# Banded attention scores of two block pairs issued back to back, with one projection bank less

## The chip, the cores and the metric

The kernel runs on one core of one Trainium2 chip. The metric is the device time of one execution in microseconds; the figure before is the median of three runs, 1133.69 us.

## The reference, cut to what matters

One decoder layer over 2048 positions of width 1024. A normalised and modulated input is projected once into the operands of two attention branches; each branch output is gated, and both go through one output projection.

```python
h = rms_norm(x, g_pre) * (1 + scale) + shift
qa, ka, va, fa, za, qb, kb, vb, zb = split(h @ w_in)
oa = forgetting_attention(qa, ka, va, fa + b_fgate) * silu(za)      # 8 heads, causal, forget-gate bias
qb, kb = rope(qb), rope(kb)
ob = sliding_window_sink_attention(qb, kb, vb, sinks) * silu(zb)    # 8 heads, 2 key heads, window 128
y = concat(oa, ob) @ w_out
x = x + gate * rms_norm(y, g_post)
```

The change lies in branch B. There, every block of 128 queries looks at its own 128 keys and the 128 before it, masked to a band of 128; a learned "sink" score joins each row's softmax.

## The kernel before, in words

Everything on TensorE is done in 16-bit pieces: an operand is split into a high and a low half, and a product is three matmuls (high by high, high by low, low by high). The order of all instructions is written by hand: each engine runs its own instructions in the order in which the program issues them, and waits where it needs another's result.

The time falls into three parts. Up to about 140 us the input is normalised, transposed and projected. From 140 to 400 us runs the **banded stage**, where branch B's attention is mixed with projections of both branches. After it come branch A's attention and the output projection.

**The filler: projection units.** `punits` is a list of small pieces of projection work. `fill(n)` (line 1185) takes the next n; before each it runs the `events` booked for that position with `at_slice`. A group of 8 units makes one 128x512 result in one bank of PSUM: 24 matmuls of 512 columns (line 361: queries of branch B, `wh_qb`, and gates, `wh_zb`), or 48 of 256 columns (line 379: values of branch A, `wh_va`). At the group's end the result is taken out by ScalarE and then VectorE: L406 and L402 for a gate, L807 and L812 for a query, L385 and L389 for values. These are put off with `after(n, f)`, which runs f at the n-th next `tick()`.

**Banks.** `bk` holds three PSUM tiles of 128x512 f32. `bank(True)` takes the one longest unused and holds it; `release` gives it back once the VectorE step is issued.

**The pairs.** A `Pair(j, i)` is two neighbouring query blocks of one pair of heads; `windows` lists 32 of them, eight for each of the four head pairs j. A pair goes through:
- `scores` (L940 to L949): 12 matmuls of 64 rows. The two heads sit in rows 0 to 63 and 64 to 127, so that two matmuls run side by side. They write a tile `pss` of two banks from the pool `ps_s`, which has one buffer.
- `maxima` (L951 to L963): VectorE masks the scores (L956), puts in the sink (L958), takes the row maximum (L961, L963). Where a head pair starts, it first fills the missing block (L955).
- `exps` (L965 to L971): ScalarE's exponentials, the last reader of `pss`.
- `turn` (L973 to L996): four transposes (L977) into `pxb`, then a split by ScalarE (L986) and VectorE (L987) and four band cuts by GpSimd (L991, L993).
- `pv` (L998 to L1015): the product with the values, L1005, into `pob` of the pool `ps_pv`, one buffer of one bank; at the next tick `out_` (L1011, VectorE) reads it out.

The loop of line 1220 goes over the pairs. In step n it issues `maxima` of pair n, some units, `turn` of pair n-1, a tick, `exps` of pair n, units, a tick, `pv` of pair n-2, units, a tick, units, and last `scores` of pair n+1.

**Two small products use a bank of `bk` in passing.** `sums` (L892) adds up the forget gates: matmuls L896 and L897, held until a copy by VectorE (L900) three units later. `const_turn` (L763) turns a table of constants: matmul L766 and a ScalarE copy (L767) at the next tick. Its place, 40 units before the stage's end, is directly behind a `pv`.

**PSUM in all.** Eight banks: ahead of the banded stage three for `bk` and five for `ps_x`; in it three for `bk`, two for `ps_s`, one each for `ps_t` and `ps_pv`, one unused; after it `bk` grows to five.

Of the kernel before, what the change touches and what calls it, by code (L numbers as in the profile page):

```python
# [10 lines left out]
F32 = mybir.dt.float32  # L11
# [8 lines left out]
P = 128  # L20
# [4 lines left out]
CH = 512  # L25
# [18 lines left out]
def hybrid_layer(  # L44
# [23 lines left out]
    PSUM = bass.MemoryType.PSUM  # L68
    dram = ctx.enter_context(tc.tile_pool(name="dram", bufs=1, space=DRAM))
    bkx = ExitStack()  # L70
    ps_bk = bkx.enter_context(tc.tile_pool(name="ps_bk", bufs=1, space=PSUM, reuse_waits="tile"))
    psx = ExitStack()
    ps_x = psx.enter_context(tc.tile_pool(name="ps_x", bufs=5, space=PSUM, reuse_waits="tile"))

    const = ctx.enter_context(tc.tile_pool(name="const", bufs=1))
# [7 lines left out]
    def sm(n, tag):  # L83
        return small.tile([P, n], F32, tag=tag, name=tag)
# [95 lines left out]
        return kap  # L180


    bk = [ps_bk.tile([P, CH], F32, name=f"bk{n}") for n in range(3)]
    held, order_ = set(), [0, 1, 2]

    def bank(hold=False):
        n = next(n for n in order_ if n not in held)
        order_.remove(n)
        order_.append(n)
        if hold:  # L190
            held.add(n)
        return n

    def release(n):
        held.discard(n)
        order_.remove(n)
        order_.append(n)
# [4 lines left out]
    def after(n, f):  # L202
        late.append([n, f])

    def tick():
        now = [f for n, f in late if n <= 1]
        late[:] = [[n - 1, f] for n, f in late if n > 1]
        for f in now:
            f()
# [534 lines left out]
    fx, abp = {}, None  # L744
# [17 lines left out]

    def const_turn():  # L763

        px = bk[bank()][:]
        PE.matmul(px[0:XR, 0:P], fx["cst"][:], identh[:], start=True, stop=True)  # L766
        after(1, lambda: A.activation(fx["crow"][64:XR, :], px[64:XR, 0:P], AF.Copy))  # L767

# [13 lines left out]
    def swa_pool(name, bufs, **kw):  # L782
        return swa.enter_context(tc.tile_pool(name=name, bufs=bufs, reuse_waits="tile", **kw))
# [94 lines left out]
    def gates():  # L878

        nf = fap.tile([P, NB, 8], F32, name="nf")  # L880
        V.tensor_scalar(nf[:], fl[:], -1.0, None, op0=ALU.mult)
        na = fap.tile([P, NB, 8], F32, name="na")
        V.tensor_tensor(na[:], fl[:], nf[:], op=ALU.min)

        def logs():
            A.activation(na[:], na[:], AF.Exp)
            A.activation(na[:], na[:], AF.Ln, bias=1.0)

        def total():
            V.scalar_tensor_tensor(nf[:], nf[:], 0.0, na[:], op0=ALU.max, op1=ALU.add)  # L890

        def sums():  # L892
            lsf = nf[:].rearrange("p t h -> p (t h)")
            held_ = bank(True)
            pc = bk[held_][:]
            PE.matmul(pc[:, 0:P], triu[:], lsf, start=True, stop=True)  # L896
            PE.matmul(pc[:, P:2 * P], ones[:], lsf, start=True, stop=True)  # L897
            yield
            cm = fap.tile([P, 2, NB, 8], F32, name="cm")
            V.tensor_copy(cm[:].rearrange("p a t h -> p (a t h)"), pc[:, 0:2 * P])  # L900
            release(held_)

            inn = na[:].rearrange("p (g r) h -> p g r h", g=4)
            blk = cm[:, 1].rearrange("p (g r) h -> p g r h", g=4)
            V.memset(inn[:, :, 0, :], 0.0)
            V.tensor_copy(inn[:, :, 1, :], blk[:, :, 0, :])
            for r in (2, 3):
                V.tensor_tensor(inn[:, :, r, :], inn[:, :, r - 1, :], blk[:, :, r - 1, :], op=ALU.add)
            yield
            tot = fap.tile([P, 4, 8], F32, name="tot")  # L910
            V.memset(tot[:, 0, :], 0.0)
            V.tensor_tensor(tot[:, 1:4, :], inn[:, 0:3, 3, :], blk[:, 0:3, 3, :], op=ALU.add)
            for g in (2, 3):
                V.tensor_tensor(tot[:, g, :], tot[:, g, :], tot[:, g - 1, :], op=ALU.add)
            yield
            V.tensor_tensor(inn, inn, tot[:].unsqueeze(2).broadcast_to([P, 4, 4, 8]), op=ALU.add)
            V.tensor_tensor(csum[:].rearrange("p h t -> p t h"), cm[:, 0], na[:],
                            op=ALU.add)

        after(1, logs)  # L920
        after(3, total)
        fx["sums"] = sums()

    ab = {}

    def qb_units(j, ci):
        def finish(stg):
            ab[j, ci] = stg

        return proj_units(f"qb{j}", ci, evac_rope(ci, finish, None))  # L930
# [128 lines left out]
    def at_slice(n, f):  # L1059
        events.setdefault(n, []).append(f)  # L1060
# [53 lines left out]
    add("qb0", qb_units(0, 1))  # L1114
    add(*others[6])
    N_PRO = len(punits)
    for n in range(4):
        at_slice(N_PRO + 20 + 3 * n, lambda: next(fx["sums"], None))
    qbs = [(f"qb{c_ // 4}", qb_units(c_ // 4, c_ % 4)) for c_ in range(2, 16)]
    n_o = 7  # L1120
    for n, (key, us) in enumerate(qbs):
# [4 lines left out]
        n_o = lim  # L1126
    N_SWA = len(punits)
    at_slice(N_SWA - 40, const_turn)
    for us in va_units(1, 2):
        add("va23", us)  # L1130
# [51 lines left out]
    windows = [Pair(j, i) for j in range(4) for i in range(0, NB, 2)]  # L1182
    pos = [0]

    def fill(n, each=None):

        for _ in range(n):
            for f in events.pop(pos[0], []):
                f()
            punits[pos[0]]()  # L1190
            pos[0] += 1
            if each:
                each()
# [8 lines left out]
    with swa_order:  # L1202
        fill(N_PRO - 4, tick2)
        psx.close()
        sws = swa_pool("sws", 2)
        ptp = swa_pool("ptp", 1)
        ps_s = swa_pool("ps_s", 1, space=PSUM)
        ps_t = swa_pool("ps_t", 1, space=PSUM)
        ps_pv = swa_pool("ps_pv", 1, space=PSUM)
        wsp = swa_pool("wsp", 2)  # L1210
        wss, wst = sm(16, "a_m"), sm(2, "wst")
        wsq = {}
        base = N_PRO
        NW = len(windows)
        windows[0].scores()
        windows[0].maxima()
        fill(2, tick2)
        windows[0].exps()
        fill(2, tick2)
        for n, wd in enumerate(windows):  # L1220
            goal = base + (N_SWA - base) * (n + 1) // NW
            todo = goal - pos[0]
            part = [todo * (m + 1) // 4 - todo * m // 4 for m in range(4)]
            tick()
            if n:
                wd.maxima()
            fill(part[0])
            if n:
                windows[n - 1].turn()
            tick()  # L1230
            if n:
                wd.exps()
            fill(part[1])
            tick()
            if n > 1:
                windows[n - 2].pv()
            fill(part[2])
            tick()
            fill(part[3])
            if n + 1 < NW:  # L1240
                windows[n + 1].scores()

            if n:
                A.activation(wsq[n - 1][:], wsq[n - 1][:], AF.Square, accum_out=wss[:, (n - 1) % 16:(n - 1) % 16 + 1])
            if n == 16:
                V.tensor_reduce(wst[:, 0:1], wss[:], axis=AX.X, op=ALU.add)
            wsq[n] = wsp.tile([P, 2 * P], F32, tag="wsq", name="wsq")
            SP.dma_start(wsq[n][:], w_out0[n // 4 * P:(n // 4 + 1) * P, n % 4 * 2 * P:(n % 4 + 1) * 2 * P])
        tick()
        fill(5)  # L1250
        windows[NW - 1].turn()
        tick()
        fill(5)
        windows[NW - 2].pv()
        tick()
        fill(6)
        windows[NW - 1].pv()
        tick()
        tick()
        A.activation(wsq[NW - 1][:], wsq[NW - 1][:], AF.Square, accum_out=wss[:, 15:16])  # L1260
        V.tensor_reduce(wst[:, 1:2], wss[:], axis=AX.X, op=ALU.add)
        wsum = sm(1, "w_mx2")
        V.tensor_reduce(wsum[:], wst[:], axis=AX.X, op=ALU.add)
# [6 lines left out]
    def fox_pool(name, bufs, **kw):  # L1270
        return fox.enter_context(tc.tile_pool(name=name, bufs=bufs, reuse_waits="tile", **kw))
# [1 line left out]
    ps_st = fox_pool("ps_st", 1, space=PSUM)  # L1273
    ps_po = fox_pool("ps_po", 1, space=PSUM)
    ps_bx = fox_pool("ps_bx", 1, space=PSUM)
    bk += [ps_bx.tile([P, CH], F32, name=f"bk{n}") for n in (3, 4)]
    order_ += [3, 4]
    foxl, foxo = ExitStack(), ExitStack()
    op_ = foxl.enter_context(tc.tile_pool(name="opa", bufs=2, reuse_waits="tile"))
    stp = foxl.enter_context(tc.tile_pool(name="stpa", bufs=3, reuse_waits="tile"))  # L1280
# [585 lines left out]
```

## Time and profile before

| what | value |
|---|---|
| median of 3 runs (lowest, highest) | 1133.69 us (1133.3, 1134.17) |
| the profiled execution's own time | 1133.33 us |
| its span, first to last instruction | 1131.6 us |
| TensorE busy | 1111.3 us, 98% |
| VectorE busy | 906.7 us, 80% |
| ScalarE busy | 657.8 us, 58% |
| GpSimd busy | 224.6 us, 20% |

PE is TensorE, PEld its weight loads, DVE is VectorE, ACT is ScalarE, POOL is GpSimd. In the rows of the timeline the first number is the start in us from the span's start, the second how long the row lasts, then come engine, source line, operation, the tiles (out<-in), the shape and, behind x, how many instructions the row merges; a bracket gives idle time of the engine before the row and what ended it. The ends of matmuls are modelled, so the pace of TensorE is read from starts. In the chain of waits a row says how long the chain stayed on one piece of work.

### The profile page before, as it was taken

The page shows a single profiled execution, that of the slowest core. Times are in us where ns is not written, and L with a number is a line of the kernel's source. Part 1 is how long each engine was busy: PE and PEld are TensorE (multiplying, and loading weights), DVE is VectorE, ACT ScalarE, POOL GpSimd, SP SyncE. Part 2 cuts the span into 40 slices and gives each one's busy share as a digit, 9 for nine tenths or more (in the row PEclk, how much of TensorE's full clock was granted, in tenths as well). Part 3 has the DMA queues.
Part 4 walks back from the last instruction along what each step waited for, and adds up shares of the span by engine and source line. Part 5 has one row for each costly group of instructions (what it writes and reads, how often), then busy time and mean ns, then how long its engine had stood idle before and what let it go on. Part 6 is the DMA issues. An engine that isn't in the chain of part 4 may idle for free.

```text
span 1131.6 us, 25123 instructions
## 1 busy us (share of the span) xinstructions
PE 1111.3 (98%) x9854; PEld 652.4 (58%) x9854; DVE 906.7 (80%) x1988; ACT 657.8 (58%) x1145; POOL 224.6 (20%) x341
## 2 busy tenths in 40 slices
PE   8899999999999999999999999999999999999997
PEld 3566555677756855555555555655555555544444
DVE  8897488878787568798998989989887998766673
ACT  3974355555555412766767677676666879533331
POOL 3111145555556410010100111001000000100000
PEclk9999999999999999999999999999999999999999
DMA  9854434413333142234232333215312246697643
GB/s 365 276 155 96 92 92 90 92 53 92 83 81 95 31 98 53 62 99 44 59 75 69 92 65 78 49 48 73 77 32 60 73 140 178 136 251 191 202 129 112
DMA packets 124365, 119.83 MB, mean 106 GB/s; under 512 B 65977, under 2 KB 101858, under 8 KB 124246
## 3 DMA queue, kind: packets, MB, share of 16 engines
q1 hardware_dynamic: 113374, 85.73, 28.4%
q0 software_dynamic: 10720, 32.46, 12.7%
q8 instruction: 77, 1.26, 0.5%
q14 instruction: 42, 0.34, 0.1%
q10 hardware_dynamic: 152, 0.04, 0.0%
HBM read 64.49 MB, written 25.18 MB: 79 GB/s over the span
## 4 chain that ended last, share of the span: by engine, by line
PE 81%; DVE 10%; DMA 4%; ACT 2%; issue 2%; POOL 0%; SPq 0%; DVEq 0%; POOLq 0%; ACTq 0%
PE bk L361 31%; PE bk L1646 13%; PE bk L379 7%; PE sta L1415 5%; PE sta L1414 5%; PE bk L1365 5%; PE poa L1440 3%; PE poa L1441 3%; PE poa L1438 3%; PE bk L854 2%; DMA wa<-in_w_ada_dram 2%; PE pss L948 2%; PE pob L1005 1%; PE px L453 1%; DVE pha L1428 1%
## 5 line engine op out<-in xcount | busy, mean ns | idle before, releaser
L1421 ACT ACTIVATE p<-sta,lift,scl_qk 128x1024 f32<-128x1024 f32 (+2 forms) x160 | 171.9, 1074 | 129.7 <-PE sta L1415 76.9
L361 PE MATMUL bk<-hT,wh_qk 128*128 128x512 f16 x768 | 196.4, 378 | 0.0
L1428 DVE TENSOR_TENSOR pha<-p,pha 128x1024 f16<-128x1024 f32 (+2 forms) x160 | 168.9, 1056 | 0.9 <-ACT pha L1425 0.9
L1646 PE MATMUL bk<-wohl,oz 128*128 128x512 f16 x744 | 163.6, 379 | 1.8 <-DVE oz L1596 1.6
L1368 DVE TENSOR_REDUCE a_m<-bk 128x1 f32<-128x512 f32 x192 | 130.2, 685 | 38.3 <-PE bk L1365 37.8
L1425 ACT ACTIVATE pha<-p 128x1024 f16<-128x1024 f32 (+2 forms) x160 | 147.9, 924 | 4.8
L1646 PEld LDWEIGHTS <-oz 128*128 128x128 f16 x744 | 70.6, 98 | 85.3 <-DVE oz L1596 2.6
L1438 PE MATMUL poa<-vt,pha 128*128 128x65 f16 x1088 | 116.3, 193 | 0.4 <-DVE ona L1447 0.4
L1440 PE MATMUL poa<-vt,pha 128*128 128x64 f16 x1088 | 116.3, 194 | 0.0
L1441 PE MATMUL poa<-vt,pha 128*128 128x65 f16 x1088 | 115.9, 192 | 0.4 <-DVE pha L1428 0.4
L361 PEld LDWEIGHTS <-wh_qk 128*128 128x128 f16 x768 | 71.8, 97 | 73.2 <-issue 1.3
L1414 PE MATMUL sta<-T 128*128 128x512 f16 (+1 forms) x320 | 110.9, 346 | 1.0 <-ACT p L1421 1.0
L1365 PE MATMUL bk<-T 66*128 66x512 f16 (+2 forms) x320 | 110.4, 348 | 0.5 <-DMA T<-stq 0.3
L1438 PEld LDWEIGHTS <-pha 128*128 128x128 f16 x1088 | 101.6, 96 | 14.4 <-DVE ona L1447 0.6
L1415 PE MATMUL sta<-T 69*128 69x512 f16 (+1 forms) x320 | 109.8, 348 | 0.0
L1440 PEld LDWEIGHTS <-pha 128*128 128x128 f16 x1088 | 100.9, 97 | 11.7
L1441 PEld LDWEIGHTS <-pha 128*128 128x128 f16 x1088 | 100.8, 99 | 0.6 <-DVE pha L1428 0.5
L361 PE MATMUL bk<-hT,wh_za 128*128 128x512 f16 x384 | 100.4, 378 | 0.0
L361 PE MATMUL bk<-hT,wh_zb 128*128 128x512 f16 x384 | 92.1, 379 | 0.0
L379 PE MATMUL bk<-wh_va,hT 128*128 128x256 f16 x768 | 91.9, 273 | 0.0
L361 PE MATMUL bk<-hT,wh_qb 128*128 128x512 f16 x384 | 91.2, 379 | 0.0
L404 POOL DMA_DIRECT2D z_d<-tz x32 | 17.7, 554 | 342.3 <-DVE tz L402 255.1
(462 smaller groups left out, 1956.8 us busy)
## 6 DMA issues: line engine op xcount, KB each, us to landing
hT<-in_x_dram SPq DMA_DIRECT2D x20, 512.0 KB
wa<-in_w_ada_dram SPq DMA_DIRECT2D x16, 512.0 KB
z_d<-tz POOLq DMA_DIRECT2D x32, 256.0 KB, 3.2
T<-z_d SPq DMA_DIRECT2D x16, 512.0 KB
T<-stq SPq DMA_DIRECT2D x60, 128.0 KB
out_dram<-hT SPq DMA_DIRECT2D x15, 512.0 KB
xt<-in_x_dram SPq DMA_DIRECT2D x12, 512.0 KB
qs<-qf SPq DMA_DIRECT2D x80, 64.0 KB
```

The costliest lines, as they stand in the source:

```text
L361: PE.matmul(ps, whl[:, a, k, :], hT[ci][:, b, k, :], start=(k == 0 and n == 0), stop=(k == KT - 1 and n == 2))
L379: PE.matmul(ps[:, (u % 2) * 2 * P:(u % 2 + 1) * 2 * P], hT[ci][:, a, k, u * P:(u + 1) * P], wv[p][:, b, k, :], start=(k == 0 and n == 0), ...
L1365: PE.matmul(mx[:, :w], T[0:XM, 0, i * P:(i + 1) * P], T[0:XM, 2, pc * CH:pc * CH + w], start=True, stop=True)
L1414: PE.matmul(self.st[:, o:o + w], T[:, 3, kb_], T[:, 1, qc], start=True, stop=False)
L1415: PE.matmul(self.st[:, o:o + w], T[0:XR, 2, kb_], T[0:XR, 0, qc], start=False, stop=not diag)
L1421: A.activation(self.p32[:, :self.w], self.st[:, :self.w], AF.Exp, scale=scl[f"qk{self.hd}"][:], bias=lift[:])
L1425: A.activation(self.ph[:, 0, :self.w], self.p32[:, :self.w], AF.Copy)
L1428: V.tensor_tensor(self.ph[:, 1, :self.w], self.p32[:, :self.w], self.ph[:, 0, :self.w], op=ALU.subtract)
L1438: PE.matmul(po[:, u, :], ph[:, 0, pq], vt[:, b, hd, 0:65], start=(self.first and n == 0 and u == 0), stop=False)
L1440: PE.matmul(po[:, u, 0:64], ph[:, 0, pq], vt[:, b, hd, 65:VW], start=False, stop=False)
L1441: PE.matmul(po[:, u, :], ph[:, 1, pq], vt[:, b, hd, 0:65], start=False, stop=(self.last and n == len(self.blocks) - 1))
L1646: PE.matmul(py, self.hl[:, i, k, :], w_slot(8 * j + k)[:, cc], start=(k == 0 and m_ == 0), stop=(k == KT - 1 and m_ == 2))
```

## The change

`ps_s` gets two buffers, so two `pss` tiles exist, and the scores of two pairs are issued one right after the other: pairs 0 and 1 ahead of the loop, and at the end of each odd step n the pairs n+1 and n+2. The two more banks come from the unused one and from `bk`, which has two banks in the banded stage; its third, `bk1`, is a tile of a pool of its own, closed where the stage begins and opened anew behind it. `sums` and `const_turn` no longer take a bank of `bk`, but a tile `pc` in the one buffer of `ps_pv`. The two matmuls of `sums` move three units later, to the place where their copy was, and the copy follows at once.

```diff
+    b2x, psx = ExitStack(), ExitStack()
+    ps_b2 = b2x.enter_context(tc.tile_pool(name="ps_b2", bufs=1, space=PSUM, reuse_waits="tile"))
...
-    bk = [ps_bk.tile([P, CH], F32, name=f"bk{n}") for n in range(3)]
+    bk = [(ps_bk if n != 1 else ps_b2).tile([P, CH], F32, name=f"bk{n}") for n in range(3)]
...
     def const_turn():
-        px = bk[bank()][:]
+        px = fx["pc"]()[:]
         PE.matmul(px[0:XR, 0:P], fx["cst"][:], identh[:], start=True, stop=True)
         after(1, lambda: A.activation(fx["crow"][64:XR, :], px[64:XR, 0:P], AF.Copy))
...
         def sums():
             lsf = nf[:].rearrange("p t h -> p (t h)")
-            held_ = bank(True)
-            pc = bk[held_][:]
+            pc = fx["pc"]()[:]
             PE.matmul(pc[:, 0:P], triu[:], lsf, start=True, stop=True)
             PE.matmul(pc[:, P:2 * P], ones[:], lsf, start=True, stop=True)
-            yield
             cm = fap.tile([P, 2, NB, 8], F32, name="cm")
             V.tensor_copy(cm[:].rearrange("p a t h -> p (a t h)"), pc[:, 0:2 * P])
-            release(held_)
...
-    for n in range(4):
-        at_slice(N_PRO + 20 + 3 * n, lambda: next(fx["sums"], None))
+    for n in range(3):
+        at_slice(N_PRO + 23 + 3 * n, lambda: next(fx["sums"], None))
...
         psx.close()
+        assert 1 not in held, held
+        order_.remove(1)
+        b2x.close()
...
-        ps_s = swa_pool("ps_s", 1, space=PSUM)
+        ps_s = swa_pool("ps_s", 2, space=PSUM)
...
+        fx["pc"] = lambda: ps_pv.tile([P, 2 * P], F32, tag="pv", name="pc")
...
         windows[0].scores()
+        windows[1].scores()
         windows[0].maxima()
...
-            if n + 1 < NW:
-                windows[n + 1].scores()
+            if n % 2:
+                for wn in windows[n + 1:n + 3]:
+                    wn.scores()
...
-    bk += [ps_bx.tile([P, CH], F32, name=f"bk{n}") for n in (3, 4)]
-    order_ += [3, 4]
+    bk[1:] = [ps_bx.tile([P, CH], F32, name="bk1"), bk[2], *(ps_bx.tile([P, CH], F32, name=f"bk{n}") for n in (3, 4))]
+    order_ += [1, 3, 4]
```

More of the change, by code (lines that the diff above doesn't have):

```diff
@@ L71, in hybrid_layer @@
     ps_bk = bkx.enter_context(tc.tile_pool(name="ps_bk", bufs=1, space=PSUM, reuse_waits="tile"))
-    psx = ExitStack()
+    b2x, psx = ExitStack(), ExitStack()
+    ps_b2 = b2x.enter_context(tc.tile_pool(name="ps_b2", bufs=1, space=PSUM, reuse_waits="tile"))
     ps_x = psx.enter_context(tc.tile_pool(name="ps_x", bufs=5, space=PSUM, reuse_waits="tile"))
```

## The prediction, made before the result was known

> **What bounds the kernel now.** I read the page first: its span, the busy shares and the chain of work that ended last.
>
> ```profile
> span 1131.6 us, 25123 instructions
> PE 1111.3 (98%) x9854; PEld 652.4 (58%) x9854; DVE 906.7 (80%) x1988; ACT 657.8 (58%) x1145; POOL 224.6 (20%) x341
> PE 81%; DVE 10%; DMA 4%; ACT 2%; issue 2%; POOL 0%; SPq 0%; DVEq 0%; POOLq 0%; ACTq 0%
> ```
>
> TensorE sets the time, VectorE comes second. Then the stretches of the banded stage, the only place where the order of work changes; the columns are the span, busy time (and instructions) of PE, PEld, DVE, ACT and POOL, the granted clock, the DMA share and GB/s.
>
> ```profile
> 139.50:200.00 60.50, 60.50 (x481) 31.99 (x480) 50.27 (x123) 32.27 (x101) 30.04 (x44) 1.00 0.45 97
> 200.00:400.00 200.00, 199.79 (x2026) 139.90 (x2025) 153.75 (x343) 106.19 (x341) 108.47 (x156) 1.00 0.31 75
> ```
>
> In 260.5 us TensorE is idle for 0.2. So a microsecond less of its work is one gained, and a microsecond in which it is made to wait is one lost. VectorE, busy for 50.3 of the first 60.5 us, does its steps late. That is why I then looked in the timeline for when it finishes with each tile for which TensorE will now have to wait.
>
> **Part 1, scores of two pairs together.** From the timeline, and from the chain of waits for the pace of single matmuls:
>
> ```profile
> 277.46 1.03 PE L361 MATMUL bk<-hT,wh_qb 128*128 128x512 f16 x4
> 278.42 0.83 PE L948 MATMUL pss<-kst,stb 64*128 64x256 f16 x12
> 279.19 0.60 PE L361 MATMUL bk<-hT,wh_qb 128*128 128x512 f16 x2
> ```
> ```profile
> 268.01 2.62 PE bk L379 x24
> 321.60 3.24 PE bk L361 x15
> ```
>
> A matmul of 512 columns takes 3.24/15 = 0.216 us, one of 256 columns 2.62/24 = 0.109. Four of the former from 277.46 end at 278.32; the scores begin at 278.42, so going over to 64 rows costs 0.10. Twelve scores, two side by side, are six times 0.109 = 0.65; the next projection begins 0.77 after them, so going back costs 0.12. A group takes 0.85 us with both changes, about 0.2 of it. Thirty-two groups become sixteen: 16 times 0.2 = 3.2 us go. Bounds: nothing, if the step to another tile costs as much, or all of 0.2; I take 0.2, since nothing changes form between the two pairs. The odd pair's matmuls and weight loads move ahead of some nine units, a transpose group and a `pv` on TensorE's queue; they issue no DMA and pass no other queue.
>
> [...] The rows measure the very change of mode that goes, so their 0.2 stands.
>
> **Part 2, a second buffer of `pss`.** Scores wait for the exponentials of the pair before no more. Those waits are small; the last column is idle time before, in us:
>
> ```profile
> L948 PE MATMUL pss<-kst,stb 64*128 64x256 f16 x360 | 25.2, 271 | 0.2
> ```
>
> So 0.2 us are gained.
>
> **Part 3, `sums` in the buffer of `pv`.** `ps_pv` has one buffer, and the matmuls of `sums`, moved from ahead of the first `pv` to three units later, must now wait until VectorE has read that `pv` out (L1011). TensorE, then VectorE:
>
> ```profile
> 158.61 0.39 PE L896 MATMUL bk<-nf,triu 128*128 128x128 f32 x2
> 159.06 0.81 PE L361 MATMUL bk<-hT,wh_qb 128*128 128x512 f16 x3
> 159.70 0.69 PE L1005 MATMUL pob<-vb,ptb 128*128 128x64 f16 x18
> 160.23 2.11 PE L361 MATMUL bk<-hT,wh_qb 128*128 128x512 f16 x9
> 162.17 1.46 PE L361 MATMUL bk<-hT,wh_zb 128*128 128x512 f16 x6
> ```
> ```profile
> 160.47 0.29 DVE L255 TENSOR_REDUCE w_mx<-mxr 128x1 f32<-128x128 f32 x1 [0.86 <-DMA mxr<-mx_d]
> 163.34 0.42 DVE L1011 TENSOR_TENSOR on<-pob,b_ri 128x256 f32<-128x256 f32 x1
> 163.67 0.41 DVE L900 COPY cm<-bk 128x256 f32<-128x256 f32 x1
> ```
>
> The new place of the matmuls is two units (six matmuls, 1.30) behind 160.23, at 161.53. There TensorE comes 0.2 earlier for the one pair joined by then and 0.45 earlier because `sums` (158.61 to 159.06) is behind it, and 0.65 later for the scores of pair 3, now done: 161.53 again. The readout ends at 163.76, and nothing of TensorE makes it late: VectorE starts anew at 160.47 when a DMA lands. TensorE waits 2.2, with the semaphore 2.3 us, and the units, scores and transposes queued behind wait with it. Bounds: 0, if VectorE were on time, to some 3, if it falls back further. I take 2.3. VectorE's copy, which followed at 163.67, comes after the matmuls, at 164.3: 0.65 later, and all VectorE steps queued behind it too.
>
> **Part 4, two banks instead of three.** A group now needs the bank of the group two before, and so its VectorE step. I went through the groups of the stage; in four places it comes late or within 0.3 us of it.
>
> ```profile
> 169.35 2.11 PE L361 MATMUL bk<-hT,wh_qb 128*128 128x512 f16 x9
> 211.77 1.47 PE L379 MATMUL bk<-wh_va,hT 128*128 128x256 f16 x12
> 302.63 0.82 PE L379 MATMUL bk<-wh_va,hT 128*128 128x256 f16 x6
> 385.63 3.98 PE L379 MATMUL bk<-wh_va,hT 128*128 128x256 f16 x35
> 389.89 3.44 PE L379 MATMUL bk<-wh_va,hT 128*128 128x256 f16 x30
> ```
> ```profile
> 170.02 0.68 DVE L812 SCALAR_TENSOR_TENSOR qc<-bk,cosT 128x512 f32<-128x512 f32 x1
> 211.00 0.68 DVE L812 SCALAR_TENSOR_TENSOR qc<-bk,cosT 128x512 f32<-128x512 f32 x1
> 301.62 0.74 DVE L389 SCALAR_TENSOR_TENSOR vt<-bk,vt 128x256 f16<-128x256 f32 x2
> 389.93 0.29 DVE L255 TENSOR_REDUCE w_mx<-mxr 128x1 f32<-128x128 f32 x1 [6.38 <-DMA mxr<-mx_d]
> 391.44 0.75 DVE L389 SCALAR_TENSOR_TENSOR vt<-bk,vt 128x256 f16<-128x256 f32 x2
> ```
>
> At 169.35 the step ends at 170.70, 1.35 too late. But by part 3 TensorE comes there at 169.35 + 2.74 (its wait and the matmuls of `sums`) - 0.85 (pair 3's old group) = 171.24, VectorE at 170.70 + 0.65 = 171.35: 0.15 is left. At 211.77 it ends 0.09 ahead, but there TensorE comes about 1.6 later by part 3 and VectorE 0.65; at 302.63 it ends 0.27 ahead: nothing at either. In the last place thirty of 35 matmuls and 18 of the next 30 fill a bank, so a group starts at 389.89 + 18 times 0.109 = 391.85; the bank it needs is read out until 392.19, since VectorE sat waiting for a DMA. With the semaphore, 0.4. Part 4 costs 0.55; bounds 0 and, if 0.4 came at three more groups, 1.75.
>
> **Part 5, `const_turn` in the buffer of `pv`.**
>
> ```profile
> 351.26 0.86 PE L1005 MATMUL pob<-vb,ptb 128*128 128x64 f16 x24
> 351.96 0.23 PE L766 MATMUL bk<-identh,cst 128*69 128x128 f16 x1
> 354.19 0.69 DVE L402 SCALAR_TENSOR_TENSOR tz<-tz,bk 128x512 f32<-128x512 f32 x1 [1.72 <-ACT tz L406]
> 354.80 0.42 DVE L1011 TENSOR_TENSOR on<-pob,b_ri 128x256 f32<-128x256 f32 x1
> ```
> ```profile
> 324.84 0.62 PE pss L948 x12
> 325.64 0.28 DVE pss L955
> ```
>
> L766 stands right behind a `pv`, whose readout is issued only at the next tick. That readout ends at 355.22: TensorE, which went on at 351.96, would go on at 355.28, 3.3 us later, with fifteen projection matmuls and two pairs of scores queued behind it. VectorE's work between 325.64 and the readout hangs, in the chain of waits, on VectorE and ScalarE alone, and begins with scores that keep their place. So what TensorE saves between the two (two joined pairs, 0.4) is swallowed by this wait, and fourteen of sixteen savings count: 2.8. Bounds: the readout as early as in the rivals' rows below, 0.7, to 3.3 + 0.65 = 4.0. I take 3.3, from the rows of this place itself.
>
> **The sum.** -2.8 - 0.2 + 2.3 + 0.55 + 3.3 = +3.15 us. The profiled execution took 1133.33 (span 1131.6 and 1.7 around it), 0.36 below the median of 1133.69. So 1136.5 by that execution, 1136.8 by the median: slower by 0.28%. About 0.2%, 2.27 us, is what a measurement can tell here.
>
> **The rivals.**
>
> ```profile
> 243.73 0.86 PE L1005 MATMUL pob<-vb,ptb 128*128 128x64 f16 x24
> 244.63 0.42 DVE L1011 TENSOR_TENSOR on<-pob,b_ri 128x256 f32<-128x256 f32 x1 [0.36 <-PE pob L1005]
> ```
> ```profile
> DVE pss L956 <- PE pss L948: 16.0, 10, 3.7
> ```
> ```profile
> 5.64 6.09 PE L541 MATMUL pm<-wa,silb 128*128 128x512 f32 x8
> 13.23 1.88 PE L541 MATMUL pm<-wa,silb 128*128 128x512 f32 x4
> ```
>
> *VectorE catches up: faster.* It waited 16.0 us for scores; half the pairs now have them a step early. If that puts it on time at both places, as at 244.63, where the readout ends 0.65 after the `pv`, `sums` waits for nothing and `const_turn` 0.7: -3.2 - 0.2 + 0.4 + 0.7 = -2.3, 1131.4 us. It decides once both waits together are under 0.7. Against it: at the two places VectorE is held by a DMA and by ScalarE, not by scores.
>
> *`const_turn` does not wait.* If the readout is issued ahead of it, or the buffer is free some other way, all sixteen pairs count: -3.2 - 0.2 + 2.3 + 0.55 = -0.55, 1133.1 us, no change that can be told. For it speaks that I see the order of the program but not how the wait is placed.
>
> *The bank is late in more groups.* With part 4 at its bound, 1138.0 us; 302.63 would show it first.
>
> *TensorE loses pace after the long wait.* At 5.64 eight matmuls start 0.79 apart, from 13.23 on 0.43: cold, the array runs at about half. A stretch like the first after the wait would cost seven times 0.36 = 2.5 us: 1139.3. [...]
>
> **How the numbers follow.** Forecast 0.47, by itself 1135.2 to 1138.0, of which a quarter lies under 1135.96; VectorE catches up 0.15; no wait in `const_turn` 0.20; late banks 0.12; pace 0.06. Slower by over 0.2% is 0.35 + 0.12 + 0.06 = 0.53; within it 0.12 + 0.18 = 0.30; faster 0.17, the first rival and the low end of the second. The range leaves out the lost pace and most of the first rival: 1131.6 to 1138.6.
>
> **What would show it.** Right: sixteen groups of 24 scores about 1.5 us long; TensorE waiting about 2 us ahead of L896 and 3 us ahead of the constants' matmul, both released by L1011; a group near 392 waiting for L389; the clock still at 1.00. Wrong: TensorE dense there (parts 3 and 5), many groups released by L402, L812 or L389 (part 4), or scores that take 0.85 us each as before (part 1).

## The result, and the profile after

The changed kernel takes 1142.88 us, median of six runs (1140.16 to 1148.13), against 1133.53 (1133.22 to 1134.17, six runs): ratio 1.0088, 95% interval 1.0075 to 1.0101. It is slower, as forecast, but by 9.35 us and not by 3.15, and outside the range. Its runs spread over 8 us, those of the kernel before over 1; the two slowest have the lowest granted clock (0.992 and 0.993), the fastest the highest (0.999).

The profiled execution took 1147.33 us. The page: span, busy shares, the granted clock over the span (a digit for each 28.6 us), the chain.

```profile
span 1145.6 us, 25094 instructions
PE 1116.2 (97%) x9854; PEld 657.8 (57%) x9854; DVE 905.8 (79%) x1988; ACT 658.1 (57%) x1145; POOL 224.4 (20%) x341
PEclk9999999999898999999999999999999999999999
PE 79%; DVE 12%; DMA 3%; issue 3%; ACT 2%; POOL 1%; DVEq 0%; POOLq 0%; SPq 0%; ACTq 0%
```

TensorE is 4.9 us longer busy although it does the same matmuls, and the clock row has two 8s in the banded stage. The first projection of branch A's queries, which follows the stage, starts at 412.90 us (before: 398.49); the rest takes the same time. So all of what this execution lost lies in the stage. The waits of TensorE there (what it waits for, total us, times, longest):

```profile
PE pc L767 <- DVE on L1009: 3.7, 1, 3.7
PE bk L380 <- DVE vt L390: 3.0, 1, 3.0
PE pc L896 <- DVE on L1009: 2.1, 1, 2.1
PE bk L380 <- DVE qc L813: 1.0, 2, 0.7
```

L1009 is the readout of `pv`, L380 a values matmul, L390 and L813 read out the bank that it needs. And the clock, in three stretches of the stage (columns as in the prediction):

```profile
164.70:168.11 3.41, 3.41 (x10) 1.24 (x9) 3.34 (x9) 2.03 (x4) 0.72 (x2) 0.50 0.12 38
308.10:314.93 6.83, 5.97 (x47) 4.85 (x48) 4.50 (x12) 3.66 (x13) 4.66 (x7) 0.50 0.59 154
362.70:369.53 6.83, 5.36 (x14) 1.97 (x14) 1.02 (x2) 1.15 (x4) 1.28 (x2) 0.50 0.22 77
```

The clock stands at 0.50 for 3.41 us behind the 2.1 us wait and for 6.83 behind each of the longer two. What that does to a matmul, from the timeline:

```profile
358.33 1.46 PE L362 MATMUL bk<-hT,wh_zb 128*128 128x512 f16 x6
359.62 0.86 PE L1003 MATMUL pob<-vb,ptb 128*128 128x64 f16 x24
364.18 0.26 PE L767 MATMUL pc<-identh,cst 128*69 128x128 f16 x1 [3.69 <-DVE on L1009]
364.23 2.77 PE L362 MATMUL bk<-hT,wh_zb 128*128 128x512 f16 x6
155.36 1.48 PE L946 MATMUL pss<-kst,stb 64*128 64x256 f16 x24
156.78 1.47 PE L362 MATMUL bk<-hT,wh_qb 128*128 128x512 f16 x6
```

Six matmuls take 1.46 us ahead of the wait and 2.77 behind it. Counted from start to start, the waits of the stage come to 10.6 us (before 0.35) and the slow matmuls to 6.8 us more than at full pace. The last two rows are a joined group: 24 scores, the next matmul 1.42 us later. One pair took 0.77 to there, two 1.54 and one more change of mode at 0.10; so by these rows a joined group is 0.2 shorter, sixteen of them 3.2 to 3.5 us. 10.6 - 0.35 + 6.8 less that makes 13.6 to 13.9 of the 14.4 us by which the stage is longer; the rest isn't placed.

### The profile page after: what moved, and what is told of

Same layout as the page of the kernel before. It is cut to its first block, busy times and chain, and to the rows that moved or that the text cites. A ratio compares the mean times of both kernels' runs of the same rounds, so it can differ in the third digit from the quotient of the medians.

```text
span 1145.6 us, 25094 instructions
## 1 busy us (share of the span) xinstructions
PE 1116.2 (97%) x9854; PEld 657.8 (57%) x9854; DVE 905.8 (79%) x1988; ACT 658.1 (57%) x1145; POOL 224.4 (20%) x341
## 4 chain that ended last, share of the span: by engine, by line
PE 79%; DVE 12%; DMA 3%; issue 3%; ACT 2%; POOL 1%; DVEq 0%; POOLq 0%; SPq 0%; ACTq 0%
PE bk L362 30%; PE bk L1650 13%; PE bk L380 6%; PE sta L1419 5%; PE sta L1418 5%; PE bk L1369 5%; PE poa L1444 3%; PE poa L1445 3%; PE poa L1442 3%; PE bk L855 2%; DMA mxr<-mx_d 1%; PE pob L1003 1%; PE pss L946 1%; DVE pha L1432 1%; PE px L454 1%
## 5 line engine op out<-in xcount | busy, mean ns | idle before, releaser
L1372 DVE TENSOR_REDUCE a_m<-bk 128x1 f32<-128x512 f32 x192 | 130.2, 685 | 38.6 <-PE bk L1369 38.1
L1442 PEld LDWEIGHTS <-pha 128*128 128x128 f16 x1088 | 101.6, 96 | 14.4 <-DVE ona L1451 0.6
L380 PE MATMUL bk<-wh_va,hT 128*128 128x256 f16 x768 | 92.7, 276 | 4.0 <-DVE vt L390 3.0
L362 PE MATMUL bk<-hT,wh_zb 128*128 128x512 f16 x384 | 94.9, 391 | 0.0
```

What stands on the lines that cost most here:

```text
L362: PE.matmul(ps, whl[:, a, k, :], hT[ci][:, b, k, :], start=(k == 0 and n == 0), stop=(k == KT - 1 and n == 2))
L380: PE.matmul(ps[:, (u % 2) * 2 * P:(u % 2 + 1) * 2 * P], hT[ci][:, a, k, u * P:(u + 1) * P], wv[p][:, b, k, :], start=(k == 0 and n == 0), ...
L1442: PE.matmul(po[:, u, :], ph[:, 0, pq], vt[:, b, hd, 0:65], start=(self.first and n == 0 and u == 0), stop=False)
```

## Experiments

The theory: each of the change's parts does what the prediction said, but a wait costs TensorE its clock besides, and the bank term is larger because of one late readout near 305. The rivals: the waits alone cost it (the clock has no price of its own); pairing itself brings TensorE to that place too early; something delays VectorE there that the change set off.

**The waits in the buffer of `pv`, one at a time.** Three kernels on the kernel before: `const_turn` alone, the same with fifteen more projection-sized matmuls into an unused bank ahead of it (work whose result nothing reads), and `sums` alone.

```
+    fx["pc"] = lambda: ps_pv.tile([P, 2 * P], F32, tag="pv", name="pc")
...
-        px = bk[bank()][:]
+        px = fx["pc"]()[:]
```

> The kernel before with one part of the change alone: the constants' matmul takes its tile from the one buffer of the pv products. Theory (waits and clock): TensorE waits about 3.3 us in front of that matmul, until the readout of the pv directly ahead of it (L1011) is done; the idle stretch also takes the clock to half for one or two windows of 3.4 us, so 3.3 plus 0 to 3.4 us: 1137 to 1140 us, with executions that differ by more than 1 us and a granted clock below 0.999 in some. Rival (the wait alone): plus 3.3 us in every execution, 1136.9, clock 0.999. Rival (the half pace comes with the paired scores): the same 1136.9.

```
+        for _ in range(15):
+            PE.matmul(fx["dm"][:], hT[3][:, 0, 0, 0:P], hT[3][:, 0, 0, :], start=True, stop=True)
         PE.matmul(px[0:XR, 0:P], fx["cst"][:], identh[:], start=True, stop=True)
...
+        fx["dm"] = swa_pool("ps_d", 1, space=PSUM).tile([P, CH], F32, name="dm")
```

> As const_pv, but fifteen extra matmuls of 512 columns (15 times 0.216 = 3.24 us) into a PSUM bank that nothing else uses stand directly ahead of the constants' matmul, so that TensorE is busy while it would wait; nothing of the computation is left out. Theory (waits and clock): the same delay of 3.3 to 3.5 us, but no loss of clock: 1136.9 to 1137.2 us in all executions, agreeing within some tenths, clock 0.999. Rival (the wait alone): no difference from const_pv in time or scatter.

```
-            held_ = bank(True)
-            pc = bk[held_][:]
+            pc = fx["pc"]()[:]
...
-            yield
...
-            release(held_)
...
-    for n in range(4):
-        at_slice(N_PRO + 20 + 3 * n, lambda: next(fx["sums"], None))
+    for n in range(3):
+        at_slice(N_PRO + 23 + 3 * n, lambda: next(fx["sums"], None))
```

> The kernel before with the other small part alone: the two matmuls of the forget-gate sums move three units later and write into the one buffer of the pv products; three banks, scores one pair at a time. Theory (waits and clock): TensorE waits about 2.2 us for the first readout (L1011 near 163.8), and 0 to 1.7 us more where the clock drops for one window: 1135.5 to 1137.5 us. Rival (VectorE lateness is only a matter of the paired order): no wait of more than 0.5 us, 1133.5 to 1134.

Against 1133.28 for the kernel before: constants 1138.13 (1136.65 to 1139.58), ratio 1.0043, interval 1.003 to 1.0056; filled 1137.23 (1136.92 to 1137.58), 1.0036 (1.0023 to 1.005); sums 1135.94 (1135.4 to 1137.75), 1.0027 (1.0017 to 1.0038). The timeline of the first, and of the filled one:

```profile
355.39 0.27 PE L766 MATMUL pc<-identh,cst 128*69 128x128 f16 x1 [3.15 <-DVE on L1011]
355.45 6.21 PE L361 MATMUL bk<-hT,wh_zb 128*128 128x512 f16 x15
361.59 0.83 PE L948 MATMUL pss<-kst,stb 64*128 64x256 f16 x12
```
```profile
352.53 3.40 PE L767 MATMUL dm<-hT 128*128 128x512 f16 x15
355.86 0.22 PE L768 MATMUL pc<-identh,cst 128*69 128x128 f16 x1
355.92 3.40 PE L361 MATMUL bk<-hT,wh_zb 128*128 128x512 f16 x15
359.25 0.83 PE L950 MATMUL pss<-kst,stb 64*128 64x256 f16 x12
```

The constants' product comes at nearly the same time in both, 355.4 and 355.9: TensorE is held until the readout either way. But idle until then, its next fifteen matmuls take 6.14 us; busy until then, 3.33. The 2.8 us are the clock's, not the wait's: from 354.30 to 361.13 it is granted at 0.50 in the first and at 1.00 in the filled one. The medians lie only 0.9 apart, because the clock isn't lost in every run: the unfilled kernel's run with the granted clock at 0.999 took 1136.65, the other four, at 0.996 or 0.997, 1137.2 to 1139.6. `sums` shows it most cleanly: five runs at 0.999 took 1135.4 to 1136.0, the two at 0.997 1137.2 and 1137.8. So the wait by itself is worth 2.4 us there and about 3.4 at `const_turn` (1136.65, a single run), which the prediction had as 2.3 and 3.3; a lost clock adds 1.5 to 2.1 us there and up to 2.9 here.

**Banks and pairing without those waits.** `sums` and `const_turn` go ahead of the stage (the control); then two banks; then pairs as well; then pairs with three banks, which projections and `pv` share.

```
-    for n in range(4):
-        at_slice(N_PRO + 20 + 3 * n, lambda: next(fx["sums"], None))
+    for n in (-8, -5, 26, 29):
+        at_slice(N_PRO + n, lambda: next(fx["sums"], None))
...
-    at_slice(N_SWA - 40, const_turn)
+    at_slice(N_PRO - 11, const_turn)
```

> Control: the kernel before with the forget-gate sums and the constants' matmul placed ahead of the banded stage (8 and 11 units before it), where they use the three projection banks as before; nothing else. All theories: within 0.5 us of before, 1133.0 to 1134.0; it is the base for the kernels that change the banks or the pairing without putting these two products into the buffer of pv.

The next adds the lines of the change on `ps_b2`, `order_` and `bk[1:]`:

> The control with two projection banks instead of three in the banded stage; scores one pair at a time, one buffer for them. Theory (two banks make TensorE wait by themselves): waits of about 1.4 us near 169 (L812), 0.4 near 392 (L389) and some tenths elsewhere, plus 1.5 to 4 us: 1135 to 1137.5. Rival (the 3.2 us wait of the changed kernel was a knock-on of the two pv waits): no wait over 0.5 us, plus at most 0.6: under 1134.2.

This one those on `ps_s` and `scores()` as well:

> The changed kernel with the forget-gate sums and the constants' matmul ahead of the banded stage instead of in the buffer of pv: paired scores and two banks are left of the change. Theory: the pairing gives 16 times 0.2 = 3.2 us and the two waits of the pv buffer are gone, the bank waits stay: early_two_banks less 3, so 1132 to 1135. Rival (the pairing brings nothing): the same time as early_two_banks.

And this one has the pairs and three banks, but no `ps_pv`:

```
-            po = ps_pv.tile([P, 4, 64], F32, tag="pv", name="pob")
+            pb = bank(True)
+            po = bk[pb][:, 0:2 * P].rearrange("p (n d) -> p n d", n=4)
...
+                release(pb)
```

> Paired scores with three projection banks: the pv products take one of these banks from their issue to their readout instead of a bank of their own; sums and constants ahead of the stage. Theory (the cost of the change lies in buffers that are late, the gain in the pairing): most of the 3.2 us is realised, 1130 to 1131.5, if no group waits more than some tenths. Rival (two banks in effect): waits of 1 us and more appear at groups that follow a late pv readout, 1132 to 1136.

The control takes 1132.91 (ratio 0.9998, 0.999 to 1.0007): moving the two early costs nothing. Two banks 1134.23 (1.001, 1.0001 to 1.0018), 1.3 more than the control. With pairs as well 1135.44 (1.0014, 1.0005 to 1.0023) and 1134.5 (1.0011, 1.0003 to 1.002), where saving sixteen changes of mode should have made it about 3 us faster. None of the three came as its theory had it. Both profiles show a wait that the unpaired kernel with two banks doesn't have; in the paired kernel with two banks:

```profile
299.76 3.19 PE L362 MATMUL bk<-hT,wh_qb 128*128 128x512 f16 x14
305.99 1.46 PE L380 MATMUL bk<-wh_va,hT 128*128 128x256 f16 x6 [3.04 <-DVE vt L390]
```

It is the wait that the changed kernel has near 306 (released by L390), and half clock follows it here too (0.50 from 305.50 to 308.91). So neither `sums` nor `const_turn` makes it, and a third bank doesn't cure it (2.7 us in the last kernel). VectorE is late. Its rows and those of the other engines, in the unpaired and in the paired kernel with two banks:

```profile
273.20 1.07 SPq L1252 DMA_DIRECT2D wsq<-in_w_out_dram  x2
273.32 0.58 POOL L240 DMA_DIRECT2D mx_d<-w_mx  x1
279.11 0.91 DVE L823 TENSOR_TENSOR qs<-qs,sinT 128x512 f32<-128x512 f32 x1
283.75 0.68 DVE L817 TENSOR_TENSOR stb<-qc,stb 128x512 f16<-128x512 f32 x1
302.73 0.74 DVE L390 SCALAR_TENSOR_TENSOR vt<-bk,vt 128x256 f16<-128x256 f32 x2
```
```profile
272.20 0.58 POOL L240 DMA_DIRECT2D mx_d<-w_mx  x1
272.74 1.06 SPq L1254 DMA_DIRECT2D wsq<-in_w_out_dram  x2
280.50 0.69 DVE L823 TENSOR_TENSOR qs<-qs,sinT 128x512 f32<-128x512 f32 x1 [2.42 <-DMA qs<-qf]
282.79 0.42 ACT L1250 ACTIVATE wsq<-wsq 128x256 f32<-128x256 f32 x1 [5.83 <-DMA wsq<-in_w_out_dram]
285.13 0.65 POOL L992 TENSOR_SCALAR_AFFINE_SELECT ptb<-fold 128x512 f16<-128x512 f16 x1
285.33 2.75 DVE L817 TENSOR_TENSOR stb<-qc,stb 128x512 f16<-128x512 f32 x1
305.19 0.74 DVE L390 SCALAR_TENSOR_TENSOR vt<-bk,vt 128x256 f16<-128x256 f32 x2
```

In the unpaired kernel the reads of `w_out` (`wsq`) go out 0.12 us ahead of the small write `mx_d` (128 numbers, the column maxima of a weight); in the paired one, 0.54 behind it, since pairing brought VectorE and GpSimd 1.1 us forward and SP only 0.5. There VectorE waits for `qs`, ScalarE 5.8 us for `wsq`, and L817, which now starts behind the first of GpSimd's four selects, takes 2.75 us instead of 0.68. From there on VectorE is late: it ends L390 at 305.93, in the unpaired kernel at 303.47. The transfers of both, between 271 and 283 us (packets, MB, share of 16 engines' time):

```profile
q1 hardware_dynamic: 480, 0.52, 17.0%
```
```profile
q1 hardware_dynamic: 472, 0.52, 44.8%
```

The same 0.52 MB on SP's queue hold the DMA engines 2.6 times as long. The changed kernel has the same: `mx_d` at 274.81, `wsq` at 275.36, VectorE waiting 2.25 us for `qs`, L817 2.74. The slow L817 isn't needed for it: in the paired kernel with three banks VectorE waits 2.35 us for `qs`, the same step takes 0.66, and TensorE still waits 2.7.

**The order of the two transfers.** To tell this from the other rival (pairing makes TensorE early, the transfer is by the way), the write is put behind the reads in paired kernels, and the reads are put behind it in the unpaired one. First, VectorE's maximum L237, which `mx_d` carries away, two units later:

```
+                if n == 1 and key == "qb3":
+                    lead -= 2
```

> Against the kernel with pairs, two banks and early sums and constants (1135.44 us; TensorE waits 5.7 us, of it 3.2 at 302.6 for a bank that VectorE reads out late): here VectorE's maximum of the weights of qb3 (L237) is issued two units later, behind the readout L1012, so that the small write mx_d<-w_mx that follows it on GpSimd starts after the reads of w_out (wsq) instead of 0.5 us before them. Theory A (those reads are slow, some 2 us a packet instead of 0.05, because they come just behind that write; they hold qs<-qf, VectorE waits 2.4 us for it and is late from there on): no slow reads near 274, no wait of VectorE for qs there, the wait near 302 under 0.8 us and no half-clock stretch: 1131.5 to 1133 us. Theory B (pairing as such brings TensorE to this place before VectorE; the slow transfer is by the way): the wait near 302 stays over 2 us, 1134.5 to 1136 us.

Then the unpaired kernel with two banks and two small transfers, into a tile that nothing reads, ahead of the reads of pair 16:

```
+            if n == 16:
+                for r in range(2):
+                    SP.dma_start(swt.tile([P, 16], F32, tag=f"dly{r}", name="dly")[:], ident[:, 0:16])
             wsq[n] = wsp.tile([P, 2 * P], F32, tag="wsq", name="wsq")
```

> Against the unpaired kernel with two banks (1134.23 us, one wait of 1.2 us at 169): two small transfers (128 x 16 elements of the identity into an unused tile) are put on SP ahead of the read of w_out of pair 16, so that these reads start some 1.1 us later, behind the write mx_d<-w_mx instead of with it. The result is the same, only this work is added. Theory A: the reads near 275 take 2 us a packet and more, VectorE waits about 2 us for qs<-qf or ScalarE for wsq, and TensorE waits 1 to 3 us for a bank near 302 without any pairing: 1135.5 to 1137.5 us. Theory B: reads as before, no wait near 302, 1133.9 to 1134.6 us.

The first edit in the changed kernel, in the paired kernel with shared banks, and in the unpaired kernel with two banks:

> The changed kernel with the maximum of the weights of qb3 two units later, as in the paired kernel of this call. Theory A: the waits of TensorE for banks at 290.8 (0.9 us) and 305.6 (3.2 us) go, to under 1 us together, and with them the half-clock stretch from 308 (6.8 us, worth 2.3 us by 0.33 of it); the waits for sums at 161 and const_turn at 360 stay with theirs: 1142.9 - 3.5 - 2.3 = 1137.1, that is 1136 to 1138.5 us. Theory B: they stay, 1142 to 1144 us.

> Pairs, with three banks that projections and pv share, early sums and constants (1134.5 us; waits 1.4 at 169, 0.5 at 212, 2.7 at 302), and the maximum of the weights of qb3 two units later. Theory A: the wait at 302 and its half-clock stretch go, 1134.5 - 2.7 - 1.2 = 1130.6, that is 1130 to 1132 us, faster than the kernel before by some 2 us. Theory B: 1133.8 to 1135 us.

> The unpaired kernel with two banks, early sums and constants (1134.23 us) and the maximum of the weights of qb3 two units later: the counterpart without pairs of the paired kernel that took 1131.51 us. If the gain of that kernel is the pairing's (sixteen changes of mode fewer, some 3 us), this one stays where its like was, 1133.3 to 1134.8 us, with one wait of 1.2 us at 169. If the later maximum by itself gives the gain, it comes to 1131 to 1132.5 us.

| kernel | as it was | with the edit | ratio to before (95%) |
|---|---|---|---|
| paired, two banks; maximum later | 1135.44 | 1131.51 (1130.87 to 1132.3) | 0.9987 (0.9978 to 0.9996) |
| paired, shared banks; maximum later | 1134.5 | 1131.79 (1130.99 to 1132.11) | 0.9989 (0.998 to 0.9998) |
| changed kernel; maximum later | 1142.88 | 1139.23 (1138.07 to 1139.61) | 1.0051 (1.0039 to 1.0064) |
| unpaired, two banks; maximum later | 1134.23 | 1134.23 (1133.23 to 1134.64) | 1.0008 (0.9999 to 1.0017) |
| unpaired, two banks; reads later | 1134.23 | 1139.88 (1138.04 to 1140.63) | 1.0055 (1.0042 to 1.0067) |

The order of the transfers decides. The paired kernel gains 3.9 us by it, the unpaired one, where the order was good already, nothing; put into the bad order, the unpaired one loses 5.65, of which 2.1 us are traced to this place. The paired kernel with the write moved, and the unpaired one with the reads moved:

```profile
272.65 1.08 SPq L1256 DMA_DIRECT2D wsq<-in_w_out_dram  x2
274.01 0.57 POOL L240 DMA_DIRECT2D mx_d<-w_mx  x1 [1.86 <-DVE w_mx L237]
279.03 0.90 DVE L823 TENSOR_TENSOR qs<-qs,sinT 128x512 f32<-128x512 f32 x1
303.12 0.83 PE L380 MATMUL bk<-wh_va,hT 128*128 128x256 f16 x6 [0.94 <-DVE vt L390]
```
```profile
273.15 0.58 POOL L240 DMA_DIRECT2D mx_d<-w_mx  x1
274.32 1.06 SPq L1255 DMA_DIRECT2D wsq<-in_w_out_dram  x2
283.56 0.42 ACT L1248 ACTIVATE wsq<-wsq 128x256 f32<-128x256 f32 x1 [5.66 <-DMA wsq<-in_w_out_dram]
303.71 0.83 PE L949 MATMUL pss<-kst,stb 64*128 64x256 f16 x12 [1.36 <-ACT sm__4347 L971]
305.99 0.27 PE L380 MATMUL bk<-wh_va,hT 128*128 128x256 f16 x1 [0.70 <-DVE vt L390]
```

And SP's transfers in the same 12 us, in the same order of kernels:

```profile
q1 hardware_dynamic: 480, 0.52, 15.8%
```
```profile
q1 hardware_dynamic: 693, 0.48, 40.8%
```

In these five runs three expectations were missed in size. In the paired kernel 0.9 us of the wait near 303 stays where under 0.8 was expected. The changed kernel came to 1139.23, not 1136 to 1138.5: of the bank waits 1.07 and 0.45 us are left (at 304.3 and 214.3), and behind `sums` and `const_turn` the clock still falls: three of the five runs have it at 0.994 to 0.997, the kernel before at 0.998 or 0.999. The unpaired kernel with late reads lost more than expected. In its profile 2.1 us lie ahead of the first projection of branch A's queries, which is the two waits shown. Another 1.6 lie behind it, where TensorE waits 2.0 us near 427 for a transfer (`stq` into `T`, L1372) that the unpaired kernel with two banks doesn't wait for; whether the late reads or the two added transfers bring that wait isn't shown. Its runs differ besides: the two at a granted clock of 0.999 took 1138.04 and 1138.10, the three at 0.997 1139.88 to 1140.63.

The two paired kernels with the later maximum, and sums and constants ahead of the stage, are the versions that beat the kernel before, by 1.5 and 1.2 us. The unpaired counterpart of the first takes 1134.23, so pairing is worth 2.7 us by medians. The prediction has 16 times 0.2 = 3.2 us for it where, as here, no wait swallows two of the savings.

## Why the prediction was wrong, point by point

The direction was right, the size was not. Two steps failed: part 4, which was mis-sized because it missed why VectorE would fall back, and the clock, which was left out of the sum.

- *Part 1, pairing:* right. Groups of 24 scores, 1.48 us each as forecast; 2.7 us by the last pair of kernels, for 3.2.
- *Part 2, the second buffer:* consistent; no wait of that kind is left. It wasn't run alone.
- *Part 3, `sums` waits for the readout:* right, 2.4 us for 2.3, the readout L1009 as the releaser.
- *Part 5, `const_turn` waits:* right, 3.4 us by the run that kept the clock for 3.3; in the changed kernel 3.85 from start to start.
- *Part 4, two banks:* this step failed, in its place and its size. "Part 4 costs 0.55", at 169 and at 392: in the changed kernel neither of the two waits came. Instead 0.46 us at 214.6, 0.9 at 290.8 and 3.2 at 305.6 (ahead of L380, 4.5 together; the prediction's bound was 1.75). The rival "late banks" named the right place ("302.63 would show it first"), where VectorE was 0.27 us ahead. What it lacked is why VectorE would fall back. For the four late places the prediction worked out how far TensorE and VectorE move; of what moves ahead with the pairs it said only that "they issue no DMA and pass no other queue". That holds for the matmuls, but not for the work of VectorE and GpSimd that moves forward with them: pairing brought GpSimd's small write ahead of SP's reads, and by the two kernels with two banks that cost VectorE some 2.5 us at this place. Of two banks by themselves the cost is 1.3 us, in the unpaired kernel as one wait of 1.2 at 169.3.
- *The clock:* "the clock still at 1.00" was to show the steps right; it fell three times. As a rival it had 0.06 and 2.5 us for one wait. The price per wait was about right (2.8 in the filled comparison), in part by luck: its 0.79 us from start to start is a mean of five starts at the slow pace, 0.85 to 1.04 apart, and two at 0.43. Wrong was to leave it out of the sum, with two waits of over 2 us forecast there: in the changed kernel the 2.24 us of waiting ahead of `sums` were enough.
- *Fourteen of sixteen savings counted, two swallowed by the wait of `const_turn`:* not tested by itself.

By medians: sums 2.7, constants 4.9 (both with the clock as it fell, about 1.7 of the 7.6), banks 1.3, pairing -2.7 and the order of the transfers 3.9 add up to 10.1; measured are 9.35. The parts were measured in different surroundings, and the 0.7 isn't resolved.

## What to carry to other kernels

An idle time of a full TensorE had two prices here, its length and, behind each of the changed kernel's waits of 2.2, 3.2 and 3.9 us, the clock; where waits like these are forecast, both belong in the sum. And when a change brings one engine's work forward, go through the transfers that are issued near each other from different queues: which now comes first may matter more than the work that was saved. If an edit gains nothing where the work did go away, look for the first step that is late against the variant without it, and swap back that one order.

## What the runs showed of the hardware

**The clock.** In each profile the granted clock changes only at whole multiples of 3.413 us from its first change; in the changed kernel that is at 11.13 us, and the first half-clock stretch begins 45 of these periods later, at 164.73. Counted in these periods (a wait from start to start, less the pace of one matmul, waits under 0.8 us left out), every one in the profiles in which TensorE waited 2.0 us or more was followed by half clock: 2.24, 2.32 and 2.35 us in the changed kernel, 2.21 and 2.74 in the kernels with `const_turn` and `sums` alone, 2.71 and 2.04 near 302 in the two paired kernels without the later maximum, 2.01 and 2.18 in the changed kernel with the later maximum. No period at full clock with less was; the largest of these held 1.95 us, in the profile of the kernel before 1.55 (11.14 to 13.12 us). The 1.95 belong to a wait of 2.2 us near 427 in the unpaired kernel with late reads, which lay across the end of a period and kept its clock. Half clock lasted one period (3.4 us) where TensorE waited 0.5 us or less within it, and two (6.8) where it waited 0.87 us or more. So waits of much the same length, 2.2 us near 427 there and 2.24 near 164 in the changed kernel, kept and lost the clock, by where they fell in the periods. Runs of one kernel that keep or lose it agree with that, but only one run of each kernel was profiled.

**Transfers.** Where the first read of `w_out` was issued 0.5 to 1.2 us behind the 128 writes of 4 bytes, the transfers held SP's queue 2.4 to 2.8 times as long as where it was issued ahead of them. At this place the write lands 6.9 to 8.7 us after its issue in every order traced, and by the semaphores in the traces several transfers of SP's queue are reported done only at about that moment. In the paired kernel with two banks the write lands at 280.20; the last transfer of `qs`, whose packets end by 274.0, is reported at 280.38, and with the write moved at 274.04. The two transfers added to the unpaired kernel have packets of 0.01 us and are reported at 281.04 and 281.20, where the write lands at 280.87. Even in the unpaired kernel in the good order the second read, issued 0.5 us behind the write, is reported at 281.46, the write landing at 281.30, but nothing on TensorE's way waits for it. Why is open: the order was tested, not the cause. The order alone doesn't fix the price of every place either. Near 167 us the kernel before has a read 2.3 us behind such a write, and none of its packets takes over 0.1 us; near 184 and 217 us it has reads 1.9 and 4.6 us behind one with packets of up to 5.7 and 4.8 us, and its TensorE doesn't wait.

**VectorE beside GpSimd.** L817, which reads two tiles of SBUF, takes 0.68 us when it starts 0.19 us ahead of the first of GpSimd's selects and 2.75 when it starts 0.20 behind it (283.75 and 285.33 above). Upstream of the second start VectorE had waited 2.4 us for `qs`, and so the order was turned round. Starts by themselves don't tell: in the kernel before, the same step (L816) takes 0.67 us when it starts 0.17 us ahead of the first select (282.53), 1.73 when 0.63 behind it (209.34) and 0.78 when 0.39 behind it (361.01). Closer starts tell as little: 0.06 and 0.05 us ahead of the first select, the step took 0.66 us in the paired kernel with three banks and 2.42 in the unpaired one with the later maximum. The latter has no wait near 302, so the slow step alone doesn't make TensorE wait.
